# A four-layer hybrid decoder trunk: Newton roots in PSUM columns, and latent attention with its normalising on ScalarE

## The chip, the cores and the metric

The kernel runs on one core of a Trainium2 chip. The core has a matrix engine (TensorE, "PE" in the profile, with its weight loads as "PEld"), VectorE ("DVE"), ScalarE ("ACT"), GpSimd ("POOL") and a queue that issues most of the DMAs (SyncE, "SP"). All work from SBUF; TensorE writes to PSUM, which is used here as eight banks of 128 x 512 words of 32 bits. The metric is the device time of one execution in microseconds, as the median of several runs. The profile comes from one execution.

## The reference

The input x is 512 positions by 1024 channels, float32. Four layers follow one another, each with a different token mixer, and each adds a normalised branch to x:

```python
for i in range(DEPTH):                     # 4 layers: s5, sliding window, latent attention, gating unit
    h = rmsnorm(x, pre_norm[i])
    y = branch_i(h, ...)
    x = x + rmsnorm(y, post_norm[i])

def rmsnorm(x, g):
    y = x * rsqrt(mean(x * x, axis=-1) + EPS)
    return y * g

def mla_branch(h, ...):                    # layer 2
    c_q, c_kv, k_rope, z = split(h @ w_in, ...)          # 768, 256, 32, 1024
    q = (rmsnorm(c_q, q_norm) @ w_uq).reshape(L, 16, 64 + 32)
    kv = (rmsnorm(c_kv, kv_norm) @ w_ukv).reshape(L, 16, 64 + 64)
    q = concat(q[..., :64], rope(q[..., 64:]))
    k = concat(kv[..., :64], rope(k_rope) shared by all heads)
    s = where(causal, (q @ k.T) * 96 ** -0.5, -1e30)     # per head, 512 x 512
    p = softmax(s)
    return ((p @ v) * silu(z)) @ w_out
```

The other branches are a diagonal state-space layer with a gated linear unit (layer 0), sliding-window attention (layer 1) and a gating unit with a layer norm over v (layer 3).

## The kernel before, in words

All matrix products of the projections are made in three passes: a weight chunk `wraw` comes by DMA (1 MB each, issued on SP), ScalarE casts it to the matmul's format (`wh`, L156), and GpSimd or VectorE subtracts to get the remainder (`wl`, L160). Activations are split likewise into `XH` and `XL`. Each product then is XH·wh, XL·wh and XH·wl. The list of chunks is fixed; `get()` hands out the next one and `ahead(n)` starts the loads and splits of later ones. Some chunks are split in four parts ("mix": GpSimd, VectorE, GpSimd, VectorE in turn; "late": all on GpSimd). Instructions recorded at L66 go through a wrapper that keeps them in the program's order on their engine; the others are put in order by a planner that goes by priorities and expected times. PSUM banks come from a pool of eight (`bank()`), and an allocation waits until one is free.

`rsqrt` (L235 on) computes 1/sqrt on VectorE. A start value comes from an integer trick on the float's bits, and three Newton steps follow, each `t = y*y*h` and `y = (t + 1.5)*y`. The tiles x, h, y and t lie in SBUF, one column of 128 values each, or four columns where four blocks are done at once.

`out_proj` is the end of each layer. It multiplies the branch by w_out for four blocks t of 128 positions and two halves n of 512 channels, and threads the norms between the matmuls in an order written out by hand. For a block: `y_stat` (sum of squares, ScalarE), `y_gain` (VectorE), `y_root`, `x_new` (the residual, VectorE), then for the next layer `x_stat` (ScalarE) with a gain product on GpSimd (`hblk`), `x_root`, `x_scale` (ScalarE), transposes on TensorE, `x_high` (XH, ScalarE) and `x_low` (XL, VectorE). The first matmuls of the next layer (`nxt`) fill TensorE at the end. The splits of two weight chunks stand in the same order on VectorE and GpSimd. Part of the first chunk's matmuls (`OutFirst.step`, one block t of twelve matmuls each) is done earlier, from inside the mixer.

Layer 2, `layer_c`, ends with a loop over 16 heads. `q_tile` makes the query projection in 18 half tiles handed out by the list `share`; its rope part is made with two products on GpSimd (L1685, L1686) and four adds into `cqT` on VectorE (L1689). For a head h, `scores` makes four blocks of score rows (widths 128 to 512) on TensorE, then VectorE adds the causal mask, writes P and takes the row maximum in one instruction (L1707), scales the maxima by minus the softmax scale (`nm`, L1710), and ScalarE takes the exponential with that bias and sums the rows (L1713). `normalise` takes the reciprocal of the sums and multiplies P on VectorE (L1721). `p_transposes` makes ten 128 x 128 transposes on TensorE (L101) and evacuates them in three copies to PT, two on ScalarE (L1738) and one on VectorE (L1736). `pv` does the value product for two heads (L1748), and VectorE multiplies by the gate (L1751). `act_split(hp)` splits the result into XH (ScalarE, L226) and XL (GpSimd, L227) for the output projection. XH's first six blocks hold the queries' input until the last q tile has read them, so these splits come after it.

The order of the loop before:

```python
normalise(h); scores(h + 1); q tiles by share[h]
if h even: pv(h // 2 - 1)
p_transposes(h)
if h == 12: ahead(1); act_split(0..3)
if h == 14: act_split(4..6)
```

The tail (normalise 15, its transposes, the last `pv` and `act_split(7)`) runs between the four `OutFirst` steps at the start of `out_proj`.

Of the kernel before, what the change touches and what calls it, by code (L numbers as in the profile page):

```python
# [47 lines left out]
def tile_hybrid_trunk(ctx: ExitStack, tc: tile.TileContext, I, out, depth=4):  # L48
# [186 lines left out]
    def rsqrt(ssum, n, scale, w=1, plus=None, dve=dve, gap=lambda: None):  # L235

        x = sm.tile([128, 4], F32, name="rs_x")[:, 0:w]
        h = sm.tile([128, 4], F32, name="rs_h")[:, 0:w]
        y = sm.tile([128, 4], F32, name="rs_y")[:, 0:w]
        t = sm.tile([128, 4], F32, name="rs_t")[:, 0:w]  # L240
# [9 lines left out]
        for _ in range(3):  # L250
            if w == 1:
                dve.scalar_tensor_tensor(out=t, in0=y, scalar=y, in1=h, op0=MUL, op1=MUL)
            else:
                dve.tensor_tensor(out=t, in0=y, in1=y, op=MUL)
                dve.tensor_tensor(out=t, in0=t, in1=h, op=MUL)
            gap()
            dve.scalar_tensor_tensor(out=y, in0=t, scalar=1.5, in1=y, op0=ADD, op1=MUL)
            gap()
# [55 lines left out]
    def out_proj(pre, x, begin, tail, emit_x, nxt):  # L314
# [4 lines left out]
        more = nxt is not None  # L319

# [17 lines left out]
        def y_root(t):  # L338
            rs[t] = rsqrt(ssq[t][:, 0:1], 1, 1.0, 1, ssq[t][:, 1:2], dve_)
# [13 lines left out]
        def x_root(t):  # L353
            rs[t] = rsqrt(sss[t][:, 0:1], 1, 1.0, 1, sss[t][:, 1:2], dve_)
# [140 lines left out]
    def layer_a():  # L495
# [46 lines left out]
        idle_bt = bank()  # L542
# [67 lines left out]
        def x_root(j, w=1):  # L610
            if w == 1:
                return rsqrt(ss[:, 0, j:j + 1], 1, 1.0, 1, ss[:, 1, j:j + 1], gap=drain)
# [931 lines left out]
    def layer_c(tiles, pre, open_right, close):  # L1544
# [43 lines left out]
        def stat(i, n):  # L1588
# [3 lines left out]
            rs[i] = rsqrt(bt[:, 0:4], 4, 1.0 / n, 4)  # L1592
# [67 lines left out]
        def q_tile(c, i, halves=(0, 1)):  # L1660
# [17 lines left out]
            if i == 0:  # L1678
# [8 lines left out]
                for hh in range(4):  # L1687
                    sl = slice(32 * hh, 32 * hh + 32)
                    dve.tensor_tensor(out=qTs[2 * c + hh // 2][64:96, hh % 2, :], in0=qr[sl, :], in1=sw[sl, :], op=ADD)  # L1689
# [7 lines left out]
        def scores(h):  # L1697
            qT = qTs[h // 2]
            mx = sc_.tile([128, 4], F32, name="mx")
# [6 lines left out]
            for n in (3, 2, 0, 1):  # L1706
                dve.tensor_tensor_reduce(out=P[n][:], in0=where[n], in1=mask[:, 384 - 128 * n:512], scale=1.0,  # L1707
                                         scalar=-3e38, op0=ADD, op1=MAX, accum_out=mx[:, n:n + 1])
            nm = sc_.tile([128, 4], F32, name="nm")
            dve.tensor_scalar(out=nm[:], in0=mx[:], scalar1=-scale, scalar2=None, op0=MUL)  # L1710
            sums = sc_.tile([128, 4], F32, name="sums")
            for n in (3, 2, 0, 1):
                act.activation(out=P[n][:], in_=P[n][:], func=AF.Exp, scale=scale, bias=nm[:, n:n + 1],  # L1713
# [3 lines left out]
        def normalise(h):  # L1717
            sums = sms.pop(h)
            dve.reciprocal(out=sums[:], in_=sums[:])
            for n in range(4):  # L1720
                dve.tensor_scalar(out=Ps[h][n][:], in0=Ps[h][n][:], scalar1=sums[:, n:n + 1], scalar2=None, op0=MUL)  # L1721

        def p_transposes(h):
            P = Ps.pop(h)
            PT = c2.tile([128, 10, 128], F32, name="PT", bufs=2)
            for i, kbs in enumerate(((0,), (1, 3), (2,))):
# [8 lines left out]
                if i == 1:  # L1735
# [308 lines left out]
```

## Time and profile before

| what | value |
|---|---|
| three runs | 1017.02, 1018.6, 1020.38 us; median 1018.6 |
| the profiled execution | 1017.59 us, with a span of 1015.6 us |
| granted TensorE clock, mean | 0.978 |
| busy, share of the span | TensorE 94%, VectorE 65%, ScalarE 48%, GpSimd 42% |
| the chain that ended last | TensorE 68%, VectorE 19%, ScalarE 5%, GpSimd 3% |
| instructions | 14293 |

The layers lie one after another in the span: the state-space layer up to about 264 us, its projection until 330, the window attention with its projection until about 530, the latent attention until about 768 with its heads from about 635 on, its projection until 825, the gating unit to the end. "Busy" of TensorE contains pipelined matmuls, so a busy TensorE can still be slower than its best; the granted clock says how much of full speed it was allowed. In a row of a group, the number after x is the count, then come the busy time in us, the mean duration of one in ns, and the idle time of the engine just before, with what ended it. In a row of the timeline come the start, the duration, engine, line, operation, output<-inputs, sizes and count.

### The profile page before, as it was taken

Reading aid. Unit: us, or ns where it says so; the run is one execution under the profiler, and the core shown is the slowest. Engines: PE = TensorE matmul, PEld = TensorE weight load, DVE = VectorE, ACT = ScalarE, POOL = GpSimd, SP = SyncE. Lnnn points to the kernel's source line nnn. Section 1 sums busy time; section 2 is a strip of 40 time slices with the busy share of each in tenths; the row PEclk is TensorE's granted clock in tenths of the full one; section 3 lists DMA queues with packets and bytes.
Section 4 is the critical chain, followed back from the end, with each engine's and each line's share of the span. In section 5 each row is a group of like instructions: output and inputs, shape, how many; then the busy total and the mean of one; then the engine's idle time right before and its main releaser. Section 6 shows DMA issues by size and latency. Waiting matters only on the chain.

```text
span 1015.6 us, 14293 instructions
## 1 busy us (share of the span) xinstructions
PE 956.1 (94%) x5295; PEld 788.3 (78%) x5295; DVE 661.3 (65%) x1505; ACT 488.6 (48%) x1083; POOL 422.2 (42%) x324
## 2 busy tenths in 40 slices
PE   6969999999989999999899999999989899999997
PEld 6858987788779788878797877687757678888785
DVE  7899787845686875677812155878885867414454
ACT  4557868534457666554533252444553643222221
POOL 6676676656443223243555333021254434421210
PEclk8979999999999999999999999999989999999999
DMA  9211112344436141222234321112026032323011
GB/s 243 73 42 42 47 39 69 139 134 107 154 131 170 44 166 42 84 82 85 83 94 123 102 56 47 47 47 84 1 83 210 1 124 84 115 93 118 17 73 63
DMA packets 69222, 90.40 MB, mean 89 GB/s; under 512 B 13592, under 2 KB 49312, under 8 KB 69024
## 3 DMA queue, kind: packets, MB, share of 16 engines
q1 hardware_dynamic: 66944, 80.76, 25.7%
q10 hardware_dynamic: 2208, 8.72, 2.4%
q8 instruction: 42, 0.69, 0.3%
q14 instruction: 28, 0.23, 0.1%
HBM read 83.44 MB, written 4.98 MB: 87 GB/s over the span
## 4 chain that ended last, share of the span: by engine, by line
PE 68%; DVE 19%; ACT 5%; issue 4%; POOL 3%; DMA 0%; ACTq 0%; DVEq 0%; SPq 0%; POOLq 0%
PE bank L66 21%; PE bank L218 8%; PE bank L217 8%; PE bank L216 8%; PE bank L1811 4%; PE bank L1813 4%; PE bank L1812 4%; PE bank L101 3%; DVE rs_t L66 2%; DVE rs_y L66 2%; DVE xt L66 2%; PE bank L1704 2%; PE bank L1748 1%; PE bank L1498 1%; DVE P L1721 1%
## 5 line engine op out<-in xcount | busy, mean ns | idle before, releaser
L160 POOL TENSOR_TENSOR wl<-wraw,wh 128x2048 fp32r<-128x2048 f32 (+3 forms) x37 | 138.4, 3748 | 247.5 <-ACT wh L156 247.5
L217 PE MATMUL bank<-XL,wh 128*128 128x512 f32 (+1 forms) x526 | 182.8, 347 | 7.7 <-DVE XL L66 7.0
L216 PE MATMUL bank<-XH,wh 128*128 128x512 f32 (+1 forms) x526 | 184.4, 352 | 0.1
L218 PE MATMUL bank<-XH,wl 128*128 128x512 f32 (+1 forms) x526 | 182.4, 347 | 1.8 <-POOL wl L160 1.8
L66 POOL TENSOR_TENSOR wl<-wraw,wh 128x512 fp32r<-128x512 f32 (+1 forms) x63 | 90.2, 1455 | 95.0 <-ACT wh L66 84.3
L217 PEld LDWEIGHTS bank<-XL,wh 128*128 128x128 f32 x526 | 100.5, 191 | 21.0 <-DVE XL L66 7.7
L218 PEld LDWEIGHTS bank<-XH,wl 128*128 128x128 f32 x526 | 100.4, 191 | 15.3 <-POOL wl L160 2.2
L66 PE MATMUL bank<-wh,XH 128*128 128x512 f32 (+1 forms) x320 | 111.2, 360 | 0.9 <-ACT g L66 0.9
L216 PEld LDWEIGHTS bank<-XH,wh 128*128 128x128 f32 x526 | 100.4, 191 | 13.1 <-ACT XH L1633 0.5
L66 PE MATMUL bank<-wl,XH 128*128 128x512 f32 (+1 forms) x320 | 108.8, 352 | 0.0
L66 PE MATMUL bank<-wh,XL 128*128 128x512 f32 (+1 forms) x320 | 108.5, 351 | 0.0
L156 ACT CAST wh<-wraw 128x2048 fp32r<-128x2048 f32 (+3 forms) x50 | 71.1, 1441 | 51.1 <-PE bank L217 21.0
L1812 PE MATMUL bank<-wl,XH 128*128 128x512 f32 x192 | 76.6, 399 | 3.8 <-DVE wl L66 3.8
L66 DVE TENSOR_TENSOR wl<-wraw,wh 128x512 fp32r<-128x512 f32 x42 | 56.1, 1366 | 34.1 <-ACT wh L66 32.3
L1811 PE MATMUL bank<-wh,XH 128*128 128x512 f32 x192 | 77.0, 401 | 0.0
L1813 PE MATMUL bank<-wh,XL 128*128 128x512 f32 x192 | 76.5, 399 | 0.0
L66 PEld LDWEIGHTS bank<-wh,XH 128*128 128x128 f32 x320 | 59.1, 190 | 9.4 <-ACT g L66 1.1
L66 PEld LDWEIGHTS bank<-wh,XL 128*128 128x128 f32 x320 | 58.7, 189 | 9.0 <-DVE XL L66 0.2
L66 PEld LDWEIGHTS bank<-wl,XH 128*128 128x128 f32 x320 | 59.3, 191 | 8.0
L66 ACT CAST wh<-wraw 128x512 fp32r<-128x512 f32 (+1 forms) x105 | 59.4, 636 | 10.8 <-DMA wraw<-in_a_w_out_dram 7.9
L1713 ACT ACTIVATE P<-P,nm 128x512 f32<-128x512 f32 (+1 forms) x64 | 35.1, 550 | 53.7 <-DVE nm L1710 53.7
L66 POOL TENSOR_TENSOR hblk<-xt,gpre 128x512 f32<-128x512 f32 x24 | 31.1, 1296 | 65.3 <-DVE xt L66 47.3
(361 smaller groups left out, 2074.4 us busy)
## 6 DMA issues: line engine op xcount, KB each, us to landing
wraw<-in_d_w_in_dram SPq DMA_DIRECT2D x12, 1024.0 KB, 5.1
wraw<-in_b_w_in_dram SPq DMA_DIRECT2D x9, 1024.0 KB, 5.0
wraw<-in_c_w_in_dram SPq DMA_DIRECT2D x8, 1024.0 KB, 5.4
wraw<-in_a_w_in_dram SPq DMA_DIRECT2D x7, 1024.0 KB, 5.9
wraw<-in_c_w_uq_dram SPq DMA_DIRECT2D x8, 576.0 KB, 4.0
wraw<-in_a_w_glu_dram SPq DMA_DIRECT2D x4, 1024.0 KB, 5.1
wraw<-in_a_w_out_dram SPq DMA_DIRECT2D x4, 1024.0 KB, 5.1
wraw<-in_b_w_out_dram SPq DMA_DIRECT2D x4, 1024.0 KB, 4.9
```

The lines of the kernel that those rows point to most:

```text
L66: return lambda *a, **k: after(f(*a, **k))
L101: pe.matmul(out_ap, lhsT=in_ap, rhs=ident[0:k, 0:k], is_transpose=True, start=True, stop=True)
L156: (act_ if c["eng"] in MIX else act).copy(h, r)
L160: es[(i + k) % len(es)].tensor_tensor(out=l, in0=r, in1=h.bitcast(F32), op=SUB)
L216: pe.matmul(out_ap, lhsT=lh, rhs=rh, start=(i == 0), stop=False)
L217: pe.matmul(out_ap, lhsT=lh, rhs=rl, start=False, stop=False)
L218: pe.matmul(out_ap, lhsT=ll, rhs=rh, start=False, stop=(i == n - 1))
L1704: pe.matmul(where[n], lhsT=qT[:, h % 2, 128 * n:128 * n + 128], rhs=kT[:, h, 0:128 * (n + 1)], start=True, stop=True)
L1713: act.activation(out=P[n][:], in_=P[n][:], func=AF.Exp, scale=scale, bias=nm[:, n:n + 1], accum_out=sums[:, n:n + 1])
L1811: pe.matmul(bt[:], lhsT=xh, rhs=H[:, k, :], start=(i == 0 and k == 0), stop=False)
L1812: pe.matmul(bt[:], lhsT=xh, rhs=L[:, k, :], start=False, stop=False)
L1813: pe.matmul(bt[:], lhsT=xl, rhs=H[:, k, :], start=False, stop=(i == 1 and k == 3))
```

## The change

It has two parts.

First, `rsqrt` takes an optional place `pb` in a PSUM bank. Where it is given, x, h and t are columns of that bank and only y stays in SBUF. The factors of the step that makes t are put in another order, so that the column in PSUM is the first input. It is given in `out_proj` (a bank `roots` is held through the projection), in layer 0's first norms (a bank `idle_rt`), in the two norms of the latent attention (in the bank that holds the sums) and in layer 3's layer norm.

Second, in the latent attention: the masked scores are written negated and scaled and the minimum is taken, so that it is the exponential's bias without a further instruction; the normalising's products go from VectorE to ScalarE; the first of the three PT copies goes from ScalarE to VectorE; the rope adds go from VectorE to GpSimd; the XL part of `act_split` for outputs 1, 3 and 7 goes from GpSimd to VectorE. The q tiles end after head 11 instead of 12, the first four output splits follow at heads 11 and 12, and two of the four `OutFirst` steps are done at heads 13 and 14. The normalising of head 15 stands ahead of the tail, and the tail has one pause less.

```diff
-    def rsqrt(ssum, n, scale, w=1, plus=None, dve=dve, gap=lambda: None):
-        x = sm.tile([128, 4], F32, name="rs_x")[:, 0:w]
-        h = sm.tile([128, 4], F32, name="rs_h")[:, 0:w]
+    def rsqrt(ssum, n, scale, w=1, plus=None, dve=dve, gap=lambda: None, pb=None):
         y = sm.tile([128, 4], F32, name="rs_y")[:, 0:w]
-        t = sm.tile([128, 4], F32, name="rs_t")[:, 0:w]
+        if pb is None:
+            x, h, t = (sm.tile([128, 4], F32, name=f"rs_{i}")[:, 0:w] for i in "xht")
+        else:
+            x, h, t = (pb[:, w * i:w * i + w] for i in range(3))
...
-                dve.scalar_tensor_tensor(out=t, in0=y, scalar=y, in1=h, op0=MUL, op1=MUL)
+                dve.scalar_tensor_tensor(out=t, in0=h, scalar=y, in1=y, op0=MUL, op1=MUL)
             else:
-                dve.tensor_tensor(out=t, in0=y, in1=y, op=MUL)
-                dve.tensor_tensor(out=t, in0=t, in1=h, op=MUL)
+                dve.tensor_tensor(out=t, in0=h, in1=y, op=MUL)
+                dve.tensor_tensor(out=t, in0=t, in1=y, op=MUL)
...
+        roots = bank()
...
-            rs[t] = rsqrt(ssq[t][:, 0:1], 1, 1.0, 1, ssq[t][:, 1:2], dve_)
+            rs[t] = rsqrt(ssq[t][:, 0:1], 1, 1.0, 1, ssq[t][:, 1:2], dve_, pb=roots[:, 8 * t:8 * t + 3])
...
-            rs[t] = rsqrt(sss[t][:, 0:1], 1, 1.0, 1, sss[t][:, 1:2], dve_)
+            rs[t] = rsqrt(sss[t][:, 0:1], 1, 1.0, 1, sss[t][:, 1:2], dve_, pb=roots[:, 8 * t + 4:8 * t + 7])
...
-        idle_bt = bank()
+        idle_bt, idle_rt = bank(), bank()
...
-                return rsqrt(ss[:, 0, j:j + 1], 1, 1.0, 1, ss[:, 1, j:j + 1], gap=drain)
+                return rsqrt(ss[:, 0, j:j + 1], 1, 1.0, 1, ss[:, 1, j:j + 1], gap=drain, pb=idle_rt[:, 4 * j:4 * j + 3])
...
-            rs[i] = rsqrt(bt[:, 0:4], 4, 1.0 / n, 4)
+            rs[i] = rsqrt(bt[:, 0:4], 4, 1.0 / n, 4, pb=bt[:, 4:16])
...
-                    dve.tensor_tensor(out=qTs[2 * c + hh // 2][64:96, hh % 2, :], in0=qr[sl, :], in1=sw[sl, :], op=ADD)
+                    pool.tensor_tensor(out=qTs[2 * c + hh // 2][64:96, hh % 2, :], in0=qr[sl, :], in1=sw[sl, :], op=ADD)
...
-                dve.tensor_tensor_reduce(out=P[n][:], in0=where[n], in1=mask[:, 384 - 128 * n:512], scale=1.0,
-                                         scalar=-3e38, op0=ADD, op1=MAX, accum_out=mx[:, n:n + 1])
-            nm = sc_.tile([128, 4], F32, name="nm")
-            dve.tensor_scalar(out=nm[:], in0=mx[:], scalar1=-scale, scalar2=None, op0=MUL)
+                dve.tensor_tensor_reduce(out=P[n][:], in0=where[n], in1=mask[:, 384 - 128 * n:512], scale=-scale,
+                                         scalar=3e38, op0=ADD, op1=ALU.min, accum_out=nm[:, n:n + 1])
...
-                act.activation(out=P[n][:], in_=P[n][:], func=AF.Exp, scale=scale, bias=nm[:, n:n + 1],
+                act.activation(out=P[n][:], in_=P[n][:], func=AF.Exp, scale=-1.0, bias=nm[:, n:n + 1],
...
-                dve.tensor_scalar(out=Ps[h][n][:], in0=Ps[h][n][:], scalar1=sums[:, n:n + 1], scalar2=None, op0=MUL)
+                act.activation(out=Ps[h][n][:], in_=Ps[h][n][:], func=AF.Copy, scale=sums[:, n:n + 1])
...
-                if i == 1:
+                if i < 2:
                     dve.tensor_copy(dst, bt[:, 0:128 * w])
...
-            split_into(XH[:, :, hp, :], XL[:, :, hp, :], zt[:, hp, :].rearrange("p (j c) -> p j c", j=4), pool)
+            split_into(XH[:, :, hp, :], XL[:, :, hp, :], zt[:, hp, :].rearrange("p (j c) -> p j c", j=4),
+                       dve if hp in (1, 3, 7) else pool)
...
-        share = [2, 1, 1, 2, 1, 1, 2, 2, 1, 1, 2, 1, 1, 0, 0]
+        share = [2, 1, 1, 2, 1, 2, 1, 2, 2, 1, 2, 1]
...
-            for _ in range(share[h]):
+            for _ in range(share[h] if h < len(share) else 0):
                 q_tile(*qs.pop(0))
+            if h == 11:
+                ahead(1)
+                act_split(0)
+                act_split(1)
+            if h == 12:
+                act_split(2)
+                act_split(3)
+            if h > 12:
+                pre.step()
             if h and h % 2 == 0:
                 pv(h // 2 - 1)
             p_transposes(h)
-            if h == 12:
-                ahead(1)
-                for hp in range(4):
-                    act_split(hp)
...
+        normalise(15)
+
         def tail():
-            normalise(15)
             p_transposes(15)
-            yield
             yield
             pv(7)
             act_split(7)
-            yield
             cr.close()
...
-            r = rsqrt(mv[:, 1:2], 1, 1.0)
+            r = rsqrt(mv[:, 1:2], 1, 1.0, pb=bank()[:, 0:3])
```

More of the change, by code (lines that the diff above doesn't have):

```diff
@@ L1698, in scores @@
             qT = qTs[h // 2]
-            mx = sc_.tile([128, 4], F32, name="mx")
+            nm = sc_.tile([128, 4], F32, name="nm")
             b02, b1_, b3 = bank(), bank(), bank()
```

## The prediction

> **What bounds the kernel now.** I read the page first, then a table of stretches, then the timeline where TensorE stands still.
>
> ```profile
> span 1015.6 us, 14293 instructions
> PE 956.1 (94%) x5295; PEld 788.3 (78%) x5295; DVE 661.3 (65%) x1505; ACT 488.6 (48%) x1083; POOL 422.2 (42%) x324
> ```
>
> TensorE works for 94% of the span, and the change adds and removes no matmul. It can gain only where TensorE stands or runs at a lower granted clock. The stretches that the change touches (columns: stretch, length, busy time of PE, PEld, DVE, ACT, POOL, granted clock, DMA share, GB/s):
>
> ```profile
> 264.00:330.00 66.00, 61.41 (x371) 53.97 (x370) 49.55 (x109) 40.95 (x74) 25.52 (x17) 0.97 0.47 142
> 460.00:530.00 70.00, 65.85 (x387) 57.76 (x386) 40.80 (x101) 33.45 (x70) 31.00 (x22) 0.98 0.21 62
> 635.00:760.00 125.00, 115.90 (x729) 88.87 (x728) 103.12 (x285) 60.80 (x177) 32.63 (x19) 0.96 0.15 53
> 780.00:825.00 45.00, 40.97 (x185) 32.47 (x183) 36.78 (x97) 25.02 (x54) 19.71 (x15) 0.96 0.24 87
> 825.00:1004.00 179.00, 176.86 (x786) 143.24 (x786) 84.35 (x151) 49.34 (x68) 48.30 (x16) 1.00 0.24 80
> ```
>
> For each I count length minus PE busy, plus PE busy times what the clock lacks of 1. The latent attention's heads (635 to 760): 9.1 + 115.9 x 0.04 = 13.7 us. The three output projections that lead into a next layer (rows 1, 2, 4): 4.6 + 1.8, 4.2 + 1.3 and 4.0 + 1.6, together 17.5 us. These 31 us are the most that can come back. Layer D (last row) has 2.1 us idle, so the root in its normalisation is worth nothing there; its 786 matmuls in 176.86 us give 0.225 us for one.
>
> Why TensorE stands in a projection: the third one, on VectorE and GpSimd, then the first two stalls of the same kind.
>
> ```profile
> 803.54 0.22 DVE L66 SCALAR_TENSOR_TENSOR rs_t<-rs_y,rs_h 128x1 f32<-128x1 f32 x1
> 803.65 5.02 POOL L66 TENSOR_TENSOR wl<-wraw,wh 128x512 fp32r<-128x512 f32 x4
> 803.79 1.17 DVE L66 SCALAR_TENSOR_TENSOR rs_y<-rs_t,rs_y 128x1 f32<-128x1 f32 x1
> ...
> 807.50 1.18 DVE L66 SCALAR_TENSOR_TENSOR rs_t<-rs_y,rs_h 128x1 f32<-128x1 f32 x1
> 808.71 0.16 DVE L66 SCALAR_TENSOR_TENSOR rs_y<-rs_t,rs_y 128x1 f32<-128x1 f32 x1
> 808.79 1.28 DVE L66 TENSOR_TENSOR XL<-bank,XH 128x512 fp32r<-128x512 f32 x2
> 809.99 1.28 DVE L66 TENSOR_TENSOR wl<-wraw,wh 128x512 fp32r<-128x512 f32 x2
> 810.73 0.65 PE L1812 MATMUL bank<-wl,XH 128*128 128x512 f32 x1 [3.78 <-DVE wl L66]
> ```
>
> ```profile
> 294.65 0.39 PE L217 MATMUL bank<-XL,wh 128*128 128x256 f32 x1 [3.64 <-DVE XL L66]
> 493.90 0.58 PE L217 MATMUL bank<-XL,wh 128*128 128x256 f32 x1 [3.39 <-DVE XL L66]
> ```
>
> A Newton step on one column takes 0.16 to 0.22 us, but 1.17 to 1.18 us while GpSimd works off four weight pieces of 1.25 us each: every step, reading two SBUF tiles, waits for one piece to end. The four late steps last from 803.79 to 808.71, 4.9 us; undisturbed they are 0.16 + 0.22 + 0.16 + 0.22 and some 0.03 between two, 0.9. So 4.0 us are lost, and XL and wl queue behind them. Two such stalls, of the first and the second projection, end on XL itself.
>
> In the heads it is the same. The first row is the normalising undisturbed, the second under GpSimd:
>
> ```profile
> 731.00 1.27 DVE L1721 TENSOR_SCALAR P<-P,sums 128x128 f32<-128x128 f32 x4
> 737.66 5.86 DVE L1721 TENSOR_SCALAR P<-P,sums 128x128 f32<-128x128 f32 x4
> 744.62 4.51 POOL L160 TENSOR_TENSOR wl<-wraw,wh 128x2048 fp32r<-128x2048 f32 x1
> 744.74 0.41 DVE L1707 CUSTOM_DVE_ANT_0 P<-bank,cmask 128x256 f32<-128x256 f32 x1
> 745.09 0.68 DVE L1736 COPY PT<-bank 128x512 f32<-128x512 f32 x1
> 745.69 3.47 DVE L1710 TENSOR_SCALAR nm<-mx 128x4 f32<-128x4 f32 x1
> 749.19 0.72 ACT L1713 ACTIVATE P<-P,nm 128x512 f32<-128x512 f32 x1 [7.34 <-DVE nm L1710]
> ```
>
> Under one 4.51 us GpSimd instruction the masked scores (one input in PSUM, one in SBUF) and the PT copy (PSUM) run at full pace, while a four-column SBUF-to-SBUF scaling waits until GpSimd ends. So an instruction with a PSUM operand and one SBUF tile passes, and the changed Newton steps have that shape.
>
> **The change part by part.**
>
> *Newton roots in PSUM.* x, h and t go to a PSUM bank; each step then reads one SBUF tile, y. Per projection 4.0 us leave the chain. First and second projection: XL comes 4.0 us earlier, so the stalls of 3.64 and 3.39 go. Late next is VectorE's own share of the weight split, two 128x512 pieces with two SBUF inputs (1.28 for both), queued behind XL and still meeting GpSimd's four. For the third: chain free at 804.7, XL until 806.0, then each piece waits for the GpSimd piece that runs; with turns of 0.64 and 1.25 they end near 806.8 and 808.7. TensorE asks for the first at 806.95 and for the second some 1.4 later (six matmuls of 0.225), a stall of 0.4 where 3.78 was. For the first two the same count gives 0.75. The clock's loss behind the stalls (1.3 to 1.8 per row) halves. That is 3.3 + 0.7, 3.0 + 0.6 and 3.4 + 0.8; I keep 10 of this 11.8, because the pieces may wait a turn more. Bounds: 0 (the steps still wait) and 17.5.
>
> What a column in PSUM costs no row shows for a written one. For a read one:
>
> ```profile
> L242 DVE TENSOR_SCALAR rs_x<-bank 128x4 f32<-128x4 f32 x2 | 0.3, 164 | 0.0
> L242 DVE TENSOR_SCALAR rs_x<-bmv 128x1 f32<-128x1 f32 x4 | 0.6, 154 | 0.1
> ```
>
> That is 10 ns more. Nine instructions per root: 0.1 us, exposed once, at the very end (y_root of the last block, nothing behind it); bounds -0.1 and, if each step took the 82 ns more by which a three-operand step (0.22) exceeds a scaling (0.14), +0.7. I take +0.1. [...]
>
> The bank held through a projection leaves seven. I count at most seven live there at once (two waiting outputs, one being summed, two transposes, the root bank, the new one), so nothing waits; if TensorE waited once for a VectorE release, it would be one 0.68 evacuation. In layer A's start the steps are threaded with other VectorE scalings that also read SBUF alone: they take over the waiting, 0.
>
> *The heads.*
>
> ```profile
> L1721 DVE TENSOR_SCALAR P<-P,sums 128x128 f32<-128x128 f32 (+1 forms) x64 | 28.3, 496 | 0.5
> L1713 ACT ACTIVATE P<-P,nm 128x512 f32<-128x512 f32 (+1 forms) x64 | 35.1, 550 | 53.7 <-DVE nm L1710 53.7
> L101 PE MATMUL bank<-ident,P 128*128 128x128 f32 x160 | 23.3, 287 | 7.3 <-DVE P L1721 7.3
> L1738 ACT COPY PT<-bank 128x512 f32<-128x512 f32 x16 | 9.1, 570 | 12.3 <-PE bank L101 12.3
> L1689 DVE TENSOR_TENSOR cqT<-qr,sw 32x512 f32<-32x512 f32 x12 | 8.2, 683 | 2.4 <-POOL qr L1686 2.3
> L1710 DVE TENSOR_SCALAR nm<-mx 128x4 f32<-128x4 f32 x16 | 6.8, 425 | 0.5
> L227 POOL TENSOR_TENSOR XL<-zt,XH 128x512 fp32r<-128x512 f32 x7 | 9.2, 1340 | 23.3 <-ACT XH L226 23.3
> L1686 POOL TENSOR_TENSOR qr<-qr,rope 128x512 f32<-128x512 f32 x3 | 3.8, 1281 | 0.0
> L66 ACT ACTIVATE hblk<-hblk,rs_y 128x512 f32<-128x512 f32 x8 | 5.6, 716 | 8.6 <-DVE rs_y L66 8.6
> ```
>
> ```profile
> 727.84 1.25 PE L101 MATMUL bank<-ident,P 128*128 128x128 f32 x10
> 728.93 2.32 PE L1704 MATMUL bank<-ckT,cqT 96*128 96x512 f32 x8
> 732.69 1.90 ACT L156 CAST wh<-wraw 128x2048 fp32r<-128x2048 f32 x1
> 733.31 2.37 PE L1748 MATMUL bank<-PT,cvs 128*64 128x512 f32 x16
> ```
>
> The first table groups the stretch's instructions (count | busy, mean ns | idle before, releaser); the second gives one head's transposes and scores, a 128x2048 cast, and the value product of two heads.
>
> VectorE loses the normalising (28.3), nm (6.8) and the rope adds (8.2 in the window), and gains 16 PT copies of 0.68 (the row at 745.09; 11) and two or three splits of about 0.7: 103.1 becomes some 73 of 125. ScalarE gains 64 scalings; the 128x512 form is the hblk row's 0.716, and the exponentials over the same widths (128 to 512) average 0.550, so I price all 64 like the exponentials, 35.1 (from below, four times 0.4 a head like VectorE's 1.27, 20), and it sheds 16 wide PT copies (9.1): 60.8 becomes 87. GpSimd gains 12 rope adds, which I price by its 1.28 row though they cover 32 partitions (15.4; from below, nothing), and sheds about 4: 33 becomes 44. No engine but TensorE is full.
>
> Two new waits. On ScalarE the normalising waits for VectorE's reciprocal; behind it stand the next exponentials, a PT copy and casts. Between a head's scores and its transposes TensorE has other heads' transposes and scores (1.25 + 2.32) and mostly a value product, a q tile or a block of the projection (2.37 or 12 x 0.225) to do, and ScalarE stood idle 53.7 us there, so 0.9 us more latency (35.1/16 = 2.2 against 1.27 undisturbed for four) is covered; without that cover, 16 x 0.9 = 14.4. On GpSimd the rope adds (5.1 per q chunk) stand ahead of the next weight split; the heads that need them come two or more later: 0.
>
> [...]
>
> Moved: the q tiles end one head earlier; the first chunk's first two blocks (24 matmuls, 5.4 us) fill heads 13 and 14, which have no q tile; with them come the next chunk's 1 MB load on SP, its cast on ScalarE (1.90) and its split on GpSimd (4.51), ahead of the splits of outputs 4 to 6. The load waits for a raw buffer freed two chunks before; hidden. TensorE needs the first chunk's split after the last q tile plus two heads' transposes and scores and one value product, 2 x 1.25 + 2 x 2.32 + 2.37 = 9.5; cast plus split plus one XL piece is 1.9 + 4.5 + 1.3 = 7.7. What remains: the splits of outputs 1 and 3, now on VectorE with two SBUF inputs, can meet the 4.51 us instruction once. I leave 5.7 of the 13.7 us in place (that 4.5, and 1.2 at a weight change): gain 8, bounds -14.4 and 13.7. The last output's split loses 12 x 0.225 = 2.7 us of matmul cover behind the last value product: +0.7, half of one 1.34 split; bounds 0 and 1.3.
>
> **Sum.** Against the profiled execution's own 1017.59 (span 1015.6 and 2.0 around it): -10 - 8 + 0.1 + 0.7 = -17.2, 1000.4. The median of the three runs is 1.0 higher; I add half of that and forecast 1001, own range 995 to 1008.
>
> **The rivals.**
> - *The root stays slow* (y, its pointer and its output remain in SBUF and still wait, or the weight pieces take over the whole wait): only the heads' 8, 1010. For it: wl queues right behind. Against: the PT copy and masked scores above pass.
> - *The lock only moves in the heads*: output splits on VectorE meet GpSimd's 4.51 us twice and the chunk's split comes late: heads gain 0, 1009.
> - *Everything comes back*: 13.7 + 13, 991. For it: ScalarE's long idle time.
> - *Nothing measurable*: 1010's and 1009's causes together, 1018.
> - *The longer scalings show in every head*: nothing covers their 0.9 us, 1000.4 + 14.4 = 1014.8. For it: the transposes already waited 7.3 us for the normalising. Against: nearly all of that wait falls where GpSimd is at work.
> - *Slower: ScalarE's order becomes a ring.* If its queue takes exponentials, reciprocal wait (behind VectorE's four masked scores, about 1.9 where the 128x256 one takes 0.41), scalings, transposes (1.1), PT copy and casts strictly in turn, a head costs 2.2 + 1.9 + 2.2 + 1.1 + 0.4 + 0.8 + 0.5 = 9.1 us against 125/16 = 7.8 now. From 7.8 + 10/16 = 8.4 it eats the roots' gain; at 9.1 the heads cost 21 more: 1028. Against: now the PT copy runs behind the next head's exponentials.
>
> **How the numbers follow.** Forecast 0.50, root stays slow 0.11, lock moves 0.13, everything 0.10, scalings show 0.04, nothing 0.06, ring 0.06. A measurement here tells 0.3%, 3 us, from no change. Faster: the first four and half of "scalings show", less a tail of 0.02: 0.84; same: the other half, "nothing" and the tail, less 0.01 for its upper end: 0.09; slower 0.07. The range leaves out "scalings show", "nothing", the ring and the far end of "everything": 990 to 1012.
>
> **What would show it.** Newton steps at 0.16 to 0.25 us under GpSimd's pieces; stalls of 3.4 to 3.8 before L217 and L1812 down under 1; the nm group gone, ScalarE near 87 us busy in the heads, transposes waiting under 3 us in all (7.3 now), clock 0.98 or more there. It is wrong if Newton steps still take 1.2, if transposes wait on ScalarE for more than 0.5 us a head, or if the heads' stretch is not at least 5 us shorter.

## The result and the profile after

The changed kernel takes 991.19 us and the kernel before took 1019.06 beside it, a ratio of 0.9721 with a 95% interval of 0.9695 to 0.9747. The 991.19 is the median of four runs, three of 989.0 to 991.39 us and one of 1550.24 at a mean granted clock of 0.556, which is left out of the ratio and on which the profile fell. All that follows is therefore read in a second set of runs of the same kernel: 990.01 us, ratio 0.9714 (0.9697 to 0.9731), its profiled execution 988.96 us.

The head of the page of the changed kernel (busy time, share of the span, instructions):

```profile
span 987.2 us, 14291 instructions
PE 945.8 (96%) x5295; PEld 780.5 (79%) x5295; DVE 620.2 (63%) x1428; ACT 510.2 (52%) x1131; POOL 444.9 (45%) x337
```

The matmuls are the same 5295. Busy PE fell by 10.3 us all the same: the mean granted clock was 0.978 in the profile before and is 0.988 here, and busy time times clock is 935 us there and 934 here.

Where the 28.4 us between the two profiled executions lie, by the start times of the same instructions in both traces:

| stretch | before | after | difference |
|---|---|---|---|
| start to the first `x_new` of the first output projection | 266.2 | 264.1 | -2.1 |
| first output projection, first `x_new` to the last block's transposes | 41.4 | 37.0 | -4.4 |
| second, the same | 40.5 | 36.1 | -4.4 |
| heads: first scores to last value product | 135.6 | 123.9 | -11.7 |
| last value product to the first `x_new` of the third projection | 14.3 | 12.8 | -1.5 |
| third output projection | 40.4 | 36.0 | -4.4 |
| layer D, and its projection to the end | 193.5 | 193.5 | 0 |

The table of stretches of the changed kernel (length, busy time of PE, PEld, DVE, ACT, POOL, granted clock, DMA share, GB/s), with ends set so that each holds nearly the work of the row of before in the same place:

```profile
261.90:323.40 61.50, 59.79 (x370) 52.56 (x369) 45.16 (x109) 40.78 (x73) 27.23 (x17) 1.00 0.52 151
453.40:519.10 65.70, 64.87 (x387) 56.70 (x386) 36.52 (x101) 33.42 (x70) 32.85 (x22) 1.00 0.24 67
623.90:735.50 111.60, 109.99 (x725) 86.09 (x724) 76.03 (x207) 79.92 (x218) 44.58 (x29) 1.00 0.15 50
755.90:796.60 40.70, 39.70 (x185) 31.28 (x183) 32.55 (x98) 25.05 (x54) 21.45 (x15) 1.00 0.31 110
796.60:975.00 178.40, 176.26 (x784) 142.86 (x784) 82.30 (x150) 49.29 (x68) 48.29 (x16) 1.00 0.24 80
```

Idle time of TensorE is now 1.7, 0.8, 1.6 and 1.0 us in the first four rows, where it was 4.6, 4.2, 9.1 and 4.0, and the clock is 1.00 in all, where it was 0.96 to 0.98. VectorE's work in the heads went from 103 to 76 us, ScalarE's from 61 to 80, GpSimd's from 33 to 45.

The third projection's root again, on VectorE and GpSimd in the order of time; the rows answer to those at 803.54 to 810.73 of before:

```profile
779.55 0.23 DVE L66 SCALAR_TENSOR_TENSOR bank<-bank,rs_y 128x1 f32<-128x1 f32 x1
779.64 5.94 POOL L66 TENSOR_TENSOR wl<-wraw,wh 128x512 fp32r<-128x512 f32 x4
779.81 0.16 DVE L66 SCALAR_TENSOR_TENSOR rs_y<-bank,rs_y 128x1 f32<-128x1 f32 x1
...
780.72 0.16 DVE L66 SCALAR_TENSOR_TENSOR rs_y<-bank,rs_y 128x1 f32<-128x1 f32 x1
780.80 1.28 DVE L66 TENSOR_TENSOR XL<-bank,XH 128x512 fp32r<-128x512 f32 x2
781.99 2.45 DVE L66 TENSOR_TENSOR wl<-wraw,wh 128x512 fp32r<-128x512 f32 x2
782.80 0.19 PEld L1819 LDWEIGHTS bank<-wl,XH 128*128 128x128 f32 x1 [0.35 <-DVE wl L66]
```

The same six steps end 1.33 us after they began, under the same four pieces of GpSimd, and not 5.3. It is so everywhere: the longest of the 96 one-column steps of either kind at L66 took 2.36 and 2.27 us in the kernel before, and 0.44 and 0.16 here. Now it is the two weight pieces of VectorE that take turns with GpSimd. Of the 2.45 us, the first piece has 0.75 and the second, which has to let a GpSimd piece pass, 1.77 (before, behind GpSimd's last piece, they took 0.64 each); two of GpSimd's four stretch from 1.25 to 1.73 us. TensorE meets this as waits of 0.35 here and 0.47 at 784.50, in place of 3.78.

The heads' groups (count | busy, mean ns of one | idle before, releaser), 624 to 740:

```profile
L1715 ACT ACTIVATE P<-P,nm 128x512 f32<-128x512 f32 (+1 forms) x64 | 35.2, 552 | 21.2 <-DVE nm L1711 21.2
L1723 ACT ACTIVATE P<-P,sums 128x128 f32<-128x128 f32 (+1 forms) x64 | 30.9, 551 | 4.1 <-DVE sums L1721 4.1
L101 PE MATMUL bank<-ident,P 128*128 128x128 f32 x160 | 20.7, 275 | 0.1
L1738 DVE COPY PT<-bank 128x512 f32<-128x512 f32 x32 | 20.6, 684 | 6.1 <-PE bank L101 6.0
L1692 POOL TENSOR_TENSOR cqT<-qr,sw 32x512 f32<-32x512 f32 x12 | 15.3, 1276 | 0.9
L227 DVE TENSOR_TENSOR XL<-zt,XH 128x512 fp32r<-128x512 f32 x2 | 5.2, 2608 | 0.0
L66 PE MATMUL bank<-wh,XL 128*128 128x512 f32 x12 | 4.8, 404 | 0.6 <-POOL XL L227 0.6
```

The 64 scalings fill what was ScalarE's idle time before the exponentials (53.7 before, 21.2 now); the transposes wait 0.1 us in all, where they waited 7.3 for P.

### The profile page after: what moved, and what is told of

Read it like the earlier page. It is cut to its first block, busy times and chain, and to the rows that moved or that the text cites. A ratio compares the mean times of both kernels' runs of the same rounds, so it can differ in the third digit from the quotient of the medians.

```text
span 1548.5 us, 14291 instructions
## 1 busy us (share of the span) xinstructions
PE 1535.4 (99%) x5295; PEld 1014.5 (66%) x5295; DVE 621.9 (40%) x1428; ACT 517.6 (33%) x1131; POOL 435.6 (28%) x337
## 4 chain that ended last, share of the span: by engine, by line
PE 98%; DVE 1%; DMA 0%; ACT 0%; issue 0%; DVEq 0%; SPq 0%; ACTq 0%
PE bank L66 37%; PE bank L217 11%; PE bank L218 11%; PE bank L216 11%; PE bank L1820 5%; PE bank L1818 5%; PE bank L1819 5%; PE bank L101 4%; PE bank L1708 4%; PE bank L1750 2%; PE bank L1501 1%; PE bank L1450 1%; PE bank L1878 1%; PE bank L1451 1%; DVE ex L66 0%; PE bank L1586 0%
## 5 line engine op out<-in xcount | busy, mean ns | idle before, releaser
L216 PE MATMUL bank<-XH,wh 128*128 128x512 f32 (+1 forms) x526 | 261.0, 498 | 0.0
L217 PE MATMUL bank<-XL,wh 128*128 128x512 f32 (+1 forms) x526 | 258.3, 491 | 0.0
L218 PE MATMUL bank<-XH,wl 128*128 128x512 f32 (+1 forms) x526 | 257.8, 490 | 0.0
L66 PE MATMUL bank<-wh,XH 128*128 128x512 f32 (+1 forms) x320 | 159.6, 512 | 0.0
L66 PE MATMUL bank<-wh,XL 128*128 128x512 f32 (+1 forms) x320 | 155.4, 501 | 0.0
L66 PE MATMUL bank<-wl,XH 128*128 128x512 f32 (+1 forms) x320 | 155.1, 500 | 0.0
L66 POOL TENSOR_TENSOR wl<-wraw,wh 128x512 fp32r<-128x512 f32 (+1 forms) x63 | 92.3, 1483 | 210.6 <-ACT wh L66 180.5
L1818 PE MATMUL bank<-wh,XH 128*128 128x512 f32 x192 | 112.0, 583 | 0.0
L1820 PE MATMUL bank<-wh,XL 128*128 128x512 f32 x192 | 110.5, 575 | 0.0
L1819 PE MATMUL bank<-wl,XH 128*128 128x512 f32 x192 | 110.4, 575 | 0.0
L66 PEld LDWEIGHTS bank<-wh,XL 128*128 128x128 f32 x320 | 75.2, 241 | 31.7 <-issue 18.3
L66 PEld LDWEIGHTS bank<-wh,XH 128*128 128x128 f32 x320 | 74.5, 240 | 30.8 <-issue 16.6
L66 PEld LDWEIGHTS bank<-wl,XH 128*128 128x128 f32 x320 | 74.9, 242 | 29.6 <-issue 16.7
L66 DVE TENSOR_TENSOR wl<-wraw,wh 128x512 fp32r<-128x512 f32 x42 | 60.2, 1465 | 72.5 <-ACT wh L66 70.9
L66 ACT CAST wh<-wraw 128x512 fp32r<-128x512 f32 (+1 forms) x105 | 59.6, 633 | 17.9 <-PE bank L66 14.2
L66 ACT ACTIVATE junk<-bank 128x512 bf16<-128x512 f32 x32 | 19.1, 597 | 135.4 <-PE bank L66 135.4
L1708 PE MATMUL bank<-ckT,cqT 96*128 96x512 f32 (+3 forms) x128 | 64.2, 682 | 0.0
```

Source lines behind the costliest of these rows:

```text
L66: return lambda *a, **k: after(f(*a, **k))
L216: pe.matmul(out_ap, lhsT=lh, rhs=rh, start=(i == 0), stop=False)
L217: pe.matmul(out_ap, lhsT=lh, rhs=rl, start=False, stop=False)
L218: pe.matmul(out_ap, lhsT=ll, rhs=rh, start=False, stop=(i == n - 1))
L1708: pe.matmul(where[n], lhsT=qT[:, h % 2, 128 * n:128 * n + 128], rhs=kT[:, h, 0:128 * (n + 1)], start=True, stop=True)
L1818: pe.matmul(bt[:], lhsT=xh, rhs=H[:, k, :], start=(i == 0 and k == 0), stop=False)
```

## The experiments

Two theories stood at the start. The first: both parts work as described, each was forecast too small, and they add up. The second: the gain above the forecast comes from somewhere that the prediction had set to nothing, above all layer A's start.

**The two parts, each alone.** First the changed kernel once more:

> The whole change once more, for a profile at full clock. Measured so far: 28 us less than before (991 against 1019), where 17 were forecast. All theories expect 0.97 of the time before. They differ in the stretches. Theory 1 (the forecast's parts, each undersized): heads' stretch (125 us before, 635 to 760) shorter by 12 to 14, the three projections together by 11 to 14. Theory 2 (the heads were sized right, the rest lies elsewhere): heads shorter by 8, projections by 10, and some 10 us come back in a stretch that the forecast left at nothing, layer A's start above all.

990.01 us, ratio 0.9714 (0.9697 to 0.9731); its profile is the one above. Then the kernel before with the roots in PSUM in all places and nothing else (`rsqrt` as in the change, and):

```diff
+        roots = bank()
...
+            rs[t] = rsqrt(ssq[t][:, 0:1], 1, 1.0, 1, ssq[t][:, 1:2], dve_, pb=roots[:, 8 * t:8 * t + 3])
...
-        idle_bt = bank()
+        idle_bt, idle_rt = bank(), bank()
...
+            r = rsqrt(mv[:, 1:2], 1, 1.0, pb=bank()[:, 0:3])
```

> Only the Newton roots go to PSUM columns, everywhere as in the change; the latent attention stays as before. Forecast: 10 us less (ratio 0.990). Theory 1: 11 to 14 us less. Theory 2: 16 to 20 us less, with several of them ahead of the first projection. Rival (the weight pieces take over the wait): within 3 us of before.

1005.63 us, 0.9864 (0.9848 to 0.9881): 13.8 us less than the 1019.4 beside it. Then the edits of latent attention alone (all of the diff from the adds of `cqT` to the tail, without the roots):

```diff
-                dve.tensor_scalar(out=Ps[h][n][:], in0=Ps[h][n][:], scalar1=sums[:, n:n + 1], scalar2=None, op0=MUL)
+                act.activation(out=Ps[h][n][:], in_=Ps[h][n][:], func=AF.Copy, scale=sums[:, n:n + 1])
...
+            if h > 12:
+                pre.step()
```

> Only the latent attention is changed, the roots stay in SBUF. Forecast: 7 us less (ratio 0.993). Theory 1: 12 to 14 us less. Theory 2: 7 to 9 us less. If this and the run with the roots alone add up to 28 us, the parts don't act on each other.

1005.1 us, 0.9861 (0.9843 to 0.9878): 14.3 us less. 13.8 + 14.3 = 28.1 of the 29.4 that the whole change brings beside them: the parts add up. The stretches of the table say it more sharply. The three projections last 37.0, 36.1 and 36.0 us with the roots alone, and from the first scores to the first `x_new` behind them it is 136.7 us with the heads' edits alone (149.9 before); both are what the whole change has. Of the roots, the ones in the output projections alone:

```diff
+        roots = bank()
...
-            rs[t] = rsqrt(sss[t][:, 0:1], 1, 1.0, 1, sss[t][:, 1:2], dve_)
+            rs[t] = rsqrt(sss[t][:, 0:1], 1, 1.0, 1, sss[t][:, 1:2], dve_, pb=roots[:, 8 * t + 4:8 * t + 7])
```

> Of the roots, only those of the four output projections go to PSUM; layer A's start, the latent attention's two norms and layer D's norm keep theirs in SBUF. Theory 1: the same as with all roots, within 1.5 us, 11 to 14 us less than before. Theory 2: at least 5 us less gain than with all roots, since layer A's start or layer D holds them.

1003.98 us, 0.9855 (0.9838 to 0.9872): 15.4 us less, a little outside the expected 11 to 14, and not to be told from all the roots together, whose interval overlaps. The three projections are 37.0, 36.1 and 36.0 us here too; what the two medians have beyond these 13.2 us lies elsewhere. Its first two projections:

```profile
266.00:327.00 61.00, 59.28 (x369) 52.12 (x368) 45.20 (x103) 40.11 (x71) 27.23 (x17) 1.00 0.48 139
459.00:524.00 65.00, 64.09 (x384) 56.03 (x383) 35.31 (x98) 33.74 (x69) 33.37 (x22) 1.00 0.25 77
```

1.7 and 0.9 us idle and the clock at 1.00: the whole of what these rows had to give, from the projections' roots alone. The other way round, the changed kernel with only these roots in PSUM:

```diff
-                return rsqrt(ss[:, 0, j:j + 1], 1, 1.0, 1, ss[:, 1, j:j + 1], gap=drain, pb=idle_rt[:, 4 * j:4 * j + 3])
+                return rsqrt(ss[:, 0, j:j + 1], 1, 1.0, 1, ss[:, 1, j:j + 1], gap=drain)
...
-            rs[i] = rsqrt(bt[:, 0:4], 4, 1.0 / n, 4, pb=bt[:, 4:16])
+            rs[i] = rsqrt(bt[:, 0:4], 4, 1.0 / n, 4)
```

> The changed kernel with the PSUM columns kept only for the roots of the output projections; layer A's start, latent attention's two roots of four columns and layer D's normalisation go back to SBUF tiles (with the new order of factors). If those three give nothing, as the prediction had it, 990 to 992, level with the changed kernel within 0.2%. If layer A's start holds the 1 to 2 us by which some of the runs' first stretch was shorter, it is 992 to 993.

991.14 us, 0.9718 (0.9698 to 0.9738): level. The second theory falls. The first stretch, to the first `x_new`, is 267.3 us in this execution, but 264.3 in that of the kernel below that changes only the normalising and touches nothing there, and 267.3 again in one that has layer A's roots in PSUM (the splits back on GpSimd, below). It varies between executions by more than the 2.1 us of the table above, which is put down to no part.

**Where the operands lie, or their order.** The change also swaps the factors (h·y·y for y·y·h). The kernel before with this alone, its tiles in SBUF:

```diff
-                dve.scalar_tensor_tensor(out=t, in0=y, scalar=y, in1=h, op0=MUL, op1=MUL)
+                dve.scalar_tensor_tensor(out=t, in0=h, scalar=y, in1=y, op0=MUL, op1=MUL)
```

> The kernel before with only the factors of the Newton step in the changed order, all columns still in SBUF. If the place in PSUM is what frees the steps: the same as before within 3 us, and steps of 1.2 us under GpSimd's pieces. If the new order of the factors does it: 11 to 14 us less, like the run with the roots alone.

1020.15 us, 1.0001 (0.999 to 1.0011). Its third projection, on VectorE, GpSimd and TensorE:

```profile
804.48 0.22 DVE L66 SCALAR_TENSOR_TENSOR rs_t<-rs_h,rs_y 128x1 f32<-128x1 f32 x1
804.60 5.02 POOL L66 TENSOR_TENSOR wl<-wraw,wh 128x512 fp32r<-128x512 f32 x4
804.74 1.17 DVE L66 SCALAR_TENSOR_TENSOR rs_y<-rs_t,rs_y 128x1 f32<-128x1 f32 x1
805.95 1.22 DVE L66 SCALAR_TENSOR_TENSOR rs_t<-rs_h,rs_y 128x1 f32<-128x1 f32 x1
...
811.67 0.50 PE L1812 MATMUL bank<-wl,XH 128*128 128x512 f32 x1 [3.77 <-DVE wl L66]
```

The steps wait as before and the stall is there in full. It is the place of the operands that counts.

**The parts of the heads.** In the changed kernel the normalising goes back to VectorE:

```diff
-                act.activation(out=Ps[h][n][:], in_=Ps[h][n][:], func=AF.Copy, scale=sums[:, n:n + 1])
+                dve.tensor_scalar(out=Ps[h][n][:], in0=Ps[h][n][:], scalar1=sums[:, n:n + 1], scalar2=None, op0=MUL)
```

> The changed kernel (990) with only the normalising's 64 products put back on VectorE; all else as changed. Theory L (the lock: the heads gained because VectorE's instructions between SBUF tiles no longer wait for GpSimd): 996 to 1002, transposes wait for P for 4 us or more again and the normalising takes far over 1.27 us where the 4.5 us weight splits run. Theory F (the heads gained because the projection's first blocks and the earlier splits fill heads 12 to 14): 990 to 993. [...]

1000.64 us, 0.9813 (0.9798 to 0.9828): 10.6 us are lost again. Its groups from 626 to 747:

```profile
L1715 ACT ACTIVATE P<-P,nm 128x512 f32<-128x512 f32 (+1 forms) x64 | 35.2, 551 | 55.0 <-DVE nm L1711 55.0
L1723 DVE TENSOR_SCALAR P<-P,sums 128x128 f32<-128x128 f32 (+1 forms) x64 | 33.7, 578 | 0.5
L101 PE MATMUL bank<-ident,P 128*128 128x128 f32 x148 | 20.3, 280 | 3.6 <-DVE P L1723 3.4
```

The transposes wait for the scaling again, 3.4 us; 2.3 us more are waits for a query's rope part and for weight pieces on VectorE. The scaling's mean of 578 ns is longer than ScalarE's 551: 11 of the 64 last 1.17 to 2.05 us, each of them while GpSimd works, and the others 0.74 at most. The same move to ScalarE alone, on the kernel before:

> The kernel before with one line changed: the softmax rows are multiplied by their reciprocal sums on ScalarE and no longer on VectorE. No other part of the change is in it (scaled maxima, copies, rope adds, splits and loop order stay). If the lock on the multiplication is what the heads lost, most of the 10.6 us that the reverse edit cost in the changed kernel comes here too: 1008 to 1012. If the gain needs the negated scores, the copies on VectorE and the new order as well (the scaling of the maxima still waits 3.47 us for GpSimd, and ScalarE still has 16 wide copies), 1013 to 1018. [...]

1010.83 us, 0.9917 (0.9898 to 0.9935), 9.2 us less by the medians. Its groups from 635 to 755:

```profile
L1713 ACT ACTIVATE P<-P,nm 128x512 f32<-128x512 f32 (+1 forms) x64 | 35.1, 551 | 23.0 <-DVE nm L1710 23.0
L1721 ACT ACTIVATE P<-P,sums 128x128 f32<-128x128 f32 (+1 forms) x64 | 31.1, 554 | 5.4 <-DVE sums L1719 5.4
L101 PE MATMUL bank<-ident,P 128*128 128x128 f32 x160 | 23.8, 286 | 4.7 <-ACT P L1721 4.3
L1710 DVE TENSOR_SCALAR nm<-mx 128x4 f32<-128x4 f32 x16 | 4.1, 257 | 0.5
```

and four scalings of it under a GpSimd instruction:

```profile
731.10 4.54 POOL L160 TENSOR_TENSOR wl<-wraw,wh 128x2048 fp32r<-128x2048 f32 x1 [1.98 <-ACT wh L156]
732.71 1.92 ACT L1721 ACTIVATE P<-P,sums 128x128 f32<-128x128 f32 x4
```

None of the 64 lasts over 0.72 us on ScalarE, whether GpSimd works or not. On VectorE, in the kernel before, 7 of them last 0.94 to 1.82 us, all begun while GpSimd works, and the others 0.48 at most. The means hide this: 496 ns on VectorE there and 554 here. One line brings 9.2 of the heads' 14.3 us by the medians, 7.4 of 13.2 by the stretch from the first scores to the first `x_new`. What it leaves, 4.3 us of transposes waiting for ScalarE, is 0.1 in the full change, where ScalarE has shed the wide copies and `nm` needs no instruction; these two were not tried apart. Next, the order of the head loop, `share` and the tail as before (the tail of the change has two pauses less, not one), all else changed:

```diff
-        share = [2, 1, 1, 2, 1, 2, 1, 2, 2, 1, 2, 1]
+        share = [2, 1, 1, 2, 1, 1, 2, 2, 1, 1, 2, 1, 1, 0, 0]
...
-            if h > 12:
-                pre.step()
```

> The changed kernel with only the order of the head loop put back: the old share of q tiles, the first four output splits and the chunk after head 12, all four first blocks in the projection, head 15's normalising and the pauses in the tail as before. Engines stay as changed. Theory L: 990 to 993. Theory F: 997 to 1003, with TensorE idle again after head 12.

994.73 us, 0.9747 (0.973 to 0.9765): between what the two theories expected, 4.7 us above the changed kernel's 990.01 and 3.4 above the next kernel's 991.33, which ran beside it. In the profiled execution only 2.1 us of this lie where the edit acts (first scores to first `x_new`, 138.8 us against 136.7). The others are 2.0 us ahead of the first `x_new` and 1.6 in layer D, where nothing was edited. Then the rope's adds back on VectorE:

```diff
-                    pool.tensor_tensor(out=qTs[2 * c + hh // 2][64:96, hh % 2, :], in0=qr[sl, :], in1=sw[sl, :], op=ADD)
+                    dve.tensor_tensor(out=qTs[2 * c + hh // 2][64:96, hh % 2, :], in0=qr[sl, :], in1=sw[sl, :], op=ADD)
```

> The changed kernel with only the 16 rope adds put back on VectorE. Both theories: little, since VectorE is busy 76 of 112 us in the heads: 989 to 993; Theory L allows up to 995, as these adds read two SBUF tiles and wait for GpSimd, with the masked scores queued behind them.

991.33 us, 0.9717 (0.9699 to 0.9734): not to be told from the changed kernel. And the output splits 1, 3 and 7 back on GpSimd:

```diff
-                       dve if hp in (1, 3, 7) else pool)
+                       pool)
```

> The changed kernel with the splits of outputs 1, 3 and 7 on GpSimd again (as before), all else kept. The prediction charged these splits on VectorE with 4.5 us for meeting the 4.51 us instruction of GpSimd. If that charge was right, this kernel is up to 4 us faster than the changed one (986 to 988). If the meeting is hidden behind the heads' other matmuls, as the trace of the changed kernel suggests (TensorE waits 0.6 us in all on XL), it is level, 989 to 992, or some 1 us slower because GpSimd gets three instructions of 1.34 us at the busiest place (992 to 993).

991.25 us, 0.9717 (0.9697 to 0.9736): level too, but out of two differences. The heads are 0.9 us shorter than in the changed kernel (123.0 against 123.9) and the stretch behind the last value product 1.2 longer (14.0 against 12.8). Put back one at a time, in the stretch from the first scores to the first `x_new`, the normalising costs 9.2 us, the order 2.1, the rope adds 0.9 and the splits 0.3, in one profiled execution each: 12.5 of the 13.2, though such effects need not add up. The copies and the negated scores were not tried alone.

**A place that the change left.** In layer D's tail of the changed kernel the same wait stands (GpSimd, VectorE, TensorE):

```profile
929.34 4.59 POOL L160 TENSOR_TENSOR wl<-wraw,wh 128x2048 fp32r<-128x2048 f32 x1 [22.39 <-ACT wh L156]
930.38 4.09 DVE L66 TENSOR_TENSOR wl<-wraw,wh 128x512 fp32r<-128x512 f32 x1 [1.48 <-issue]
934.39 0.47 DVE L1882 SCALAR_TENSOR_TENSOR sact<-bank,bsT,du 128x256 f32<-128x256 f32 x1
936.68 0.63 PE L101 MATMUL bank<-ident,sact 128*128 128x128 f32 x4 [2.14 <-DVE sact L1882]
```

VectorE's first piece of a weight chunk lasts 4.09 us where the next takes 1.35: it begins under GpSimd's 128x2048 instruction and ends 0.54 us after it. Layer D's mixing product (L1882) queues behind it, and TensorE waits for that. The kernel with that chunk wholly on GpSimd:

```diff
-    def add_out(name, third=(1, 0)):
+    def add_out(name, third=(1, 0), eng="mix"):
...
-                add(name, 512 * n, 512, 4 * i, 4, tag="x" if (n, i) == third else "", eng="mix" if n else "pool")
+                add(name, 512 * n, 512, 4 * i, 4, tag="x" if (n, i) == third else "",
+                    eng=(eng if i == 0 else "mix") if n else "pool")
...
-    add_out("d_w_out")
+    add_out("d_w_out", eng="late")
```

> The changed kernel with one weight chunk of layer D's output projection (second half of the channels, first half of the inputs) subtracted wholly on GpSimd, where GpSimd and VectorE shared it. In the changed kernel VectorE's first piece of it lasts 4.09 us beside a 4.59 us instruction of GpSimd, and the mixing products of layer D queue behind it; TensorE waits 2.14 us for them once and loses some 3.2 us between 930 and 940. If the lock is the cause here too, this kernel is 2 to 3 us faster than the changed one, 987 to 989, and the mixing product is not behind a 4 us piece. If something else paces that stretch (the transposes' own chain of ScalarE and VectorE steps), it is level, 990 to 991; if GpSimd's four pieces, ending 3 us later, are needed at once, slower, 992 or more.

988.56 us (987.06 to 988.85), ratio 0.9691 (0.9672 to 0.9711) to the kernel before: the fastest here, 2.6 us under the 991.14 and 991.25 of the two level kernels that ran beside it (989.41 to 992.45). The stretch 925 to 945, first in the changed kernel:

```profile
925.00:945.00 20.00, 17.86 (x87) 14.54 (x86) 12.37 (x16) 6.61 (x10) 7.93 (x3) 1.00 0.16 54
```

and in this one, with its GpSimd and VectorE:

```profile
925.00:945.00 20.00, 20.00 (x102) 16.70 (x101) 7.86 (x16) 7.91 (x13) 9.57 (x5) 1.00 0.16 54
...
934.39 5.03 POOL L66 TENSOR_TENSOR wl<-wraw,wh 128x512 fp32r<-128x512 f32 x4
931.00 0.88 DVE L1883 SCALAR_TENSOR_TENSOR sact<-bank,bsT,du 128x256 f32<-128x256 f32 x2 [1.58 <-PE bank L1879]
```

TensorE stands 2.1 us less in these 20 us and has nothing to wait for; layer D and its projection last 191.1 us in place of 193.5.

## Why the prediction was right, and which terms were too small

The forecast of 1001 had the sign, the mechanisms and two thirds of the gain; the measured 991 lies inside the stated range (990 to 1012), by one us, and outside the likeliest case's own (995 to 1008). What came is the rival "everything comes back", 991 with a chance of 0.10. That the range holds the result is owed to this rival; the sum itself was 10 us off.

*The roots (-10 forecast, 13.2 by the stretches, 13.8 and 15.4 alone).* Right in every step of the mechanism: steps of 0.23 and 0.16 us under GpSimd, stalls of 3.4 to 3.8 gone. Mis-sized is "the clock's loss behind the stalls halves": it went to nothing, as it comes in whole pieces behind a stall (last section) and goes with it. The counted stalls' 3.3 + 3.0 + 3.4 plus all of the clock's 1.8 + 1.3 + 1.6 would be 14.4. (Two of these terms don't follow from the count: stalls of 0.75 in place of 3.64 and 3.39 give 2.9 and 2.6, and with the halves of the clock's losses the sum is 11.3, not 11.8; the 10 that was kept doesn't hang on it.) The caution, "the pieces may wait a turn more", was not needed: VectorE's two pieces end 0.7 and 2.4 us behind XL, where the count had 0.8 and 2.7.

*A column in PSUM (+0.1).* Right. A step costs 0.23 against 0.22, the other 0.16 both times, so the rows agree with the 10 ns read off the mean of the scalings. The end of the kernel, where the cost would show, is 193.5 us in both.

*The bank, layer A, layer D's norm (0).* Right: with and without the roots there it is 990.01 and 991.14 us, intervals overlapping. The longest waits of TensorE that are left in the projections, 1.12, 0.82 and 0.97 us, end on ScalarE's `hblk` and not on a bank.

*The heads (-8 and +0.7 forecast, -11.7 and -1.5 found).* The step that failed is "I leave 5.7 of the 13.7 us in place". One split of an output on VectorE did meet GpSimd's long instruction, as said: of L227's two splits one lasts 3.90 us, the other 1.32. But TensorE waits only 0.6 us for any of these remainders, and that for one of GpSimd's, and with these splits on GpSimd the heads are 0.9 us shorter, not 4.5. What is left in the row is 1.6 us idle and no clock loss. The last output's split was charged with lost cover; the stretch behind the last value product became 1.5 us shorter instead (12.8; with the old order it is 14.3 again, with the splits back on GpSimd 14.0). The prices were close: 551 ns a scaling (550 forecast), 1276 a rope add (1.28), 684 a copy (0.68), VectorE 76 (73), GpSimd 44.6 (44); ScalarE has 80 and not 87: one behind the other, the 64 scalings fill 30.9 us and not 64 x 0.55 = 35.1; the other 3 us were not traced.

*The rivals.* "ScalarE's order becomes a ring" fell: a head takes 111.6 / 16 = 7.0 us, where the ring needed 9.1, and ScalarE is busy 80 of 111.6 us. It has a trace in the kernel with the normalising alone, though: with the wide copies still on ScalarE the transposes wait 4.3 us for it. "The longer scalings show in every head" is contradicted by 1000.64 against 990.01 and by 1010.83 against 1020.03. By themselves the scalings are slower on ScalarE, as priced (1.27 us for four on VectorE against 2.2). What decided is that VectorE's last until GpSimd is done where they begin under it (0.94 to 2.05 us for one) and stand in a queue with 103 us of work in 125, while ScalarE stood idle 53.7 us before its exponentials. The argument against this rival was read too strongly: "nearly all of that wait falls where GpSimd is at work" holds for 3.5 of the 7.3 us. Another 2.16 us, at 649.83, pass while four rope adds stand between a head's scalings on VectorE, and 1.47, at 752.07, in the head whose `nm` had waited.

*What the prediction did not see* is layer D's tail: it read "2.1 us idle" in that row and called the stretch done. That idle time was the same wait, and 2.6 us were to be had there.

## What to carry to other kernels

When a tiny VectorE instruction takes as long as a GpSimd piece (1.17 us beside 1.25 here), look at where its operands lie: a working column in PSUM, at 0.01 us a step, was worth 13 to 15 us here, and the same arithmetic in another order nothing. Price a move to a slower engine by the longest cases in the busy trace, by the queue on the engine that gives and by the idle time of the one that receives; the mean, 496 ns against 554 here, would have said no. Where TensorE's short stalls go, count the granted clock's loss behind them as gone too, in whole pieces (1.5 to 1.7 us for each stall of 3.4 to 3.8 here).

## What the runs showed of the hardware

The granted clock came back as a whole: 0.96 to 0.98 in the four rows that held the stalls, 1.00 in all of them when the stalls were gone, and 0.99 to 1.00 for part of the change alone where that part applies. The loss behind a stall has a form of its own. In the kernel before, behind the stalls that end at 294.65, 493.90 and 810.73 (columns as in the table of stretches, the clock third from the end):

```profile
295.60:298.90 3.30, 3.28 (x16) 3.05 (x15) 3.19 (x7) 1.43 (x3) 2.32 (x2) 0.50 0.35 81
299.00:302.00 3.00, 3.00 (x27) 3.00 (x27) 2.79 (x8) 1.78 (x4) 1.22 (x2) 1.00 1.08 381
493.60:496.80 3.20, 2.90 (x13) 2.90 (x14) 3.13 (x8) 2.67 (x6) 0.97 (x1) 0.50 0.02 3
811.00:814.20 3.20, 3.20 (x9) 2.35 (x9) 3.06 (x7) 0.90 (x2) 2.52 (x2) 0.50 0.51 141
```

For about 3.4 us the clock is 0.50, from 295.5, 493.5 and 810.9 on, then it is 1.00 again: some 1.7 us lost behind the first and the third of these stalls of 3.4 to 3.8 and 1.5 at the second, where the piece begins 0.4 us before TensorE does: near half as much again. After the change, with waits of 1.12 us at most in the projections, no such piece comes there (the clock is 1.00 in their rows). Behind the 2.14 us wait in layer D's tail it comes in some executions and not in others; the changed kernel first, then the one with the old order:

```profile
936.70:940.00 3.30, 3.30 (x17) 2.84 (x18) 2.69 (x6) 0.58 (x1) 0.57 (x1) 1.00 0.51 197
941.60:944.80 3.20, 3.20 (x9) 2.46 (x9) 1.93 (x4) 0.39 (x1) 0.00 (x0) 0.50 0.26 101
```

That is the 1.6 us by which layer D is longer there (195.1 us against 193.5). It is 195.0 to 195.1 in three more of the kernels above too: the two with one edit on the normalising and the one with the factors' order alone.

How long VectorE waited went in these rows by how much of GpSimd's instruction was left. VectorE's pieces of 128x512, two SBUF inputs, take turns with GpSimd's pieces of the same size (VectorE's 0.75 and 1.77 us, GpSimd's up to 1.73 in place of 1.25); one VectorE piece that begins 1.04 us after a GpSimd instruction of 4.59 us lasts 4.09 and ends 0.54 us behind it.

A GpSimd addition over 32 partitions (1276 ns) costs as much as GpSimd's product over 128 partitions of the same width (1.28 us).
